# Four quarters of weight preparation and seven weight fetches of the last product group, moved within an order written out by hand

## Chip, core and metric

One core of one Trainium2 chip. The metric is the device time of one execution in microseconds (us).

## The reference

`x` is [16, 512, 512], `router_logits` [16, 512, 8], `expert_weights` [8, 512, 2048], the output [16, 512, 2048], all f32. There are T = 8192 tokens.

```python
probs = softmax(router_logits, axis=-1)
output = zeros((16, 512, 2048))
for e in range(8):
    output += probs[:, :, e:e+1] * np.matmul(x, expert_weights[e])
```

Written as one product, the left matrix is z = (p_e * x) with 8 x 512 = 4096 columns, the right one is the eight weight matrices on top of each other. Both are rounded to f16; sums of products are kept in f32.

## The kernel before

**The products.** The kernel uses Strassen's scheme in Winograd's form, with seven products of half blocks in place of eight. At the top it has 16 pairs q of token blocks (256 rows each, an even and an odd one), two halves of the experts and two halves of the output columns. This gives seven product groups P1 to P7, each a left sum of z blocks times a right sum of weight quadrants. `product(r, q)` (`Product`, `left_of`) is group r for pair q. Each of these is again made of seven inner products in the order `STEPS = (1, 5, 6, 2, 7, 3, 4)` (L353), and an inner product is 8 matmuls of 128x512 f16. The inner operands 1, 2 and 3 of a weight group are raw blocks of it; 5, 7, 6 and 4 are differences of raw blocks. "Thirds" stages (`Thirds` L511, `by_thirds` L781) split the inner products 1 and 5 of two neighbouring pairs a third time; for that `third_sums` (L178) makes four more sums from an operand.

**The stages.** A list of stages sets the order of PE's work. The groups follow one another: P1 and P2 (stages 0 to 14), P5 and P6 (15 to 31), P7 (32 to 39, k7 = 32), P4 (40 to 47, k4 = 40), P3 (48 to 56, k3 = 48). Most stages hold two products and have 14 slots, each one inner product long (the planner counts 1.73 us); stage 48 holds one product and has 7. P4's stages and P3's from 50 on are thirds stages, in which the first four slots run in `by_thirds`. `run(stage)` goes through the slots; `at(stage, slot, make)` hangs a piece of other work in front of a slot.

**What waits for what.** Every engine works in order of its program. DVE's pieces (z operands, weight sums) lie in a queue of `Task`s with a cost in us; `slack` lets as many out after each inner product as the planner's clock for DVE allows, and `need` forces one out when PE's next operand depends on it. ACT copies PSUM results (L595 to L616, L818 to L822) and also issues the fetches of weight operands from DRAM (`fetch_w`, L162 to L164, queue q10 in the profile, 1 MB each). SP issues the loads (`sp`, L117 and L118, q1): blocks of x and p, stored z, and the "base" blocks, earlier results of 256 KB that an adding step (`post_on_base`) adds. GpSimd issues the casting weight loads, stores of weight parts, and the output's stores (`pool`, L120 and L121, q0). All DVE sums go through `tt` (L107), all matmuls through `mm` (L130). Buffers come from `wpool` (15 of 1 MB), `zpool` (8) and `hpool` (12).

**P4's loads.** A product of P4 adds to output rows that P6 and P7 wrote, so `base_at` fetches four base blocks of 256 KB for each; its z of the other expert half is loaded from `z_dram` (`ZBlock`, 1 MB), as is P3's. Loads of a stage are begun two stages ahead (`start_loads`), unless `by_hook` gives them a place.

**P3's weights.** `by_parts` (L1070) makes the seven inner operands of a group in four parts, each a quarter of the rows: `begin` casts four pieces of the raw blocks (`cast_part(22)`, four POOL loads), `go_on` nine slots later stores three of them (`keep_raw`), and `end` sixteen slots after the beginning queues the four sums with their stores (`sums_in_place` L1031). The places are (stage, slot) pairs; `spread(stage, slot, every, n)` counts n places that lie `every` slots apart. `turnover` (L1127) fetches the seven finished operands, in the order of STEPS, at the slots named, counted from the start of a stage. `load_z` (L1151) hangs the z load of a product at a place, and `make_third` (L1158) the third sums of P3's operands 1 and 5. P3's operand fetches are issued by ACT between its copies; its z loads by SP.

Of the kernel before, what the change touches and what calls it, by code (L numbers as in the profile page):

```python
# [31 lines left out]
def kernel(  # L32
# [87 lines left out]
    def pool(o, i, **how):  # L120
        note(nc.gpsimd.dma_start(out=o, in_=i, **how))  # L121
# [12 lines left out]
    def new_w():  # L134
        return wpool.tile([P, K8, NB], f16, name="w", tag="w")
# [26 lines left out]
    def fetch_w(what, kn):  # L162
        t = new_w()
        note(nc.scalar.dma_start(out=t, in_=stored[what, kn]))  # L164
        return t
# [12 lines left out]
    def third_sums(w):  # L178

        t = new_w().rearrange("p (s c) (h n) -> p s c h n", s=2, h=2)  # L180
        t = {5: t[:, 0, :, 0], 6: t[:, 0, :, 1], 7: t[:, 1, :, 0], 4: t[:, 1, :, 1]}
        b = w.rearrange("p (k c) (h n) -> p k c h n", k=2, h=2)
        tt(t[5], b[:, 0, :, 1], b[:, 0, :, 0], SUB)
        tt(t[6], b[:, 1, :, 1], t[5], SUB)
        tt(t[7], b[:, 1, :, 1], b[:, 0, :, 1], SUB)
        tt(t[4], b[:, 1, :, 0], t[6], SUB)
        return {**t, 1: b[:, 0, :, 0], 2: b[:, 1, :, 0], 3: b[:, 1, :, 1]}
# [182 lines left out]
    def flush(task):  # L370
        while task is not None and not task.done:
            queue.popleft().run()
# [6 lines left out]
    def later(cost, make, first=False):  # L379
        t = Task(cost, make)  # L380
        (queue.appendleft if first else queue.append)(t)
        return t
# [286 lines left out]
    def at(stage, slot, make):  # L669
        hooks.setdefault((stage, slot), []).append(make)  # L670

    def add(*products):
        stages.append(products)
        return len(stages) - 1
# [37 lines left out]
    def product(r, q, **how):  # L712
        left, loads = left_of(r, q)
        lefts[r, q] = left
        p = None
        if r == 1:
            def sink(tn, o):
                pool(kept_rows(q)(tn), o)
            p = Product(right[1], left, sink)
        elif r == 2:  # L720
            if q >= QK:
                base = products[1, q].o.__getitem__
            else:
                base = bases[2, q] = Base(kept_rows(q))
            p = Product(right[2], left, to_out(q, 0, 0), base)
        elif r == 5:
            bases[6, q] = m1 = Base(kept_rows(q))
            m1.task = {}

            p = Product(right[5], left, to_out(q, 1, 0))  # L730
        elif r == 6:
            m1 = bases[6, q]

            def base(tn):
                need(m1.task[tn])
                return m1.t[tn]
            p = Product(right[6], left, to_out(q, 0, 1), base)
        elif r == 7:
            base = bases[7, q] = base_of(q) if q < 14 else products[6, q].o.__getitem__
            p = Product(right[7], left, to_out(q, 1, 1), base)  # L740
        elif r == 4:
            base = bases[4, q] = Base(lambda tn: out_rows(q, 1, 1, tn))
            p = Product(right[4], left, to_out(q, 1, 0, accum_op=ADD), base)
        else:
            p = Product(right[3], left, to_out(q, 0, 1, accum_op=ADD), **how)
        p.loads = loads
        products[r, q] = p
        return p
# [150 lines left out]
    k7, k4 = ks[7], ks[4]  # L899
    xs.clear()  # L900
    k3 = add(product(3, 0))
# [129 lines left out]
    def sums_in_place(part, b, r, cost):  # L1031

        def one(p, o, x, y):
            def make():
                tt(o, x, y, SUB)
                part(p, o)
            return later(cost, make)
        one(5, b[0, 0], b[0, 1], b[0, 0])
        one(7, b[0, 1], b[1, 1], b[0, 1])
        one(6, b[1, 1], b[1, 1], b[0, 0])  # L1040
        return one(4, b[1, 0], b[1, 0], b[1, 1])
# [16 lines left out]
    def slots_after(stage, slot, n):  # L1058
        slot += n
        while slot >= 7 * len(stages[stage]):  # L1060
            slot -= 7 * len(stages[stage])
            stage += 1
        return stage, slot

    def part_of(what, kn, chunks):
        return kept_w(what, kn)[:, chunks, :]
# [3 lines left out]
    def by_parts(places, r, load, between, when):  # L1070

        for j, (stage, slot) in enumerate(places):
            b, chunks = {}, ds(2 * j, 2)

            def begin(b=b, j=j, chunks=chunks):
                flush(last_part[0])
                t = new_w()
                for i, kn in enumerate(ORDER):
                    b[kn] = t[:, ds(2 * i, 2), :]
                    load(b[kn], kn, j, chunks)  # L1080

            def go_on(b=b, chunks=chunks):
                for kn in b:
                    if kn != ODD:
                        between(b[kn], kn, chunks)

            def end(b=b, chunks=chunks):
                last_part[0] = sums_in_place(lambda p, o: pool(part_of((r, p), (0, 0), chunks), o), b, r, 0.69)
            at(*slots_after(stage, slot, 0), begin)
            if between is not None:  # L1090
                at(*slots_after(stage, slot, when[0]), go_on)
            at(*slots_after(stage, slot, when[-1]), end)

    def cast_part(q):
        def load(t, kn, j, chunks):
            k, n = kn
            pool(t, expert_weights[(q // 10 - 1) * HE + 2 * k + j // 2, ds(j % 2 * 2 * P, 2 * P),
                                   ds((q % 10 - 1) * NH + n * NB, NB)].rearrange("(c p) n -> p c n", p=P))
        return load
# [18 lines left out]
    def spread(stage, slot, every, n=4):  # L1118
        return [slots_after(stage, slot, j * every) for j in range(n)]
    by_parts(spread(k5 + 2, 4, 13), 7, load_part("t3"), None, (7,))  # L1120
    by_parts(spread(*slots_after(k5 + 2, 4, 56), 28), 4, load_p4, less_t2, (9, 20))
    by_parts([(k4 - 4, 4)] + spread(k4, 4, 26, 3), 3, cast_part(22), keep_raw, (9, 16))


    RAW = {1: (0, 0), 2: (1, 0), 3: (1, 1)}
# [1 line left out]
    def turnover(stage, slots, r, raw):  # L1127

        right[r].w = {}

        def fetch(p):
            if p in RAW:
                right[r].w[p] = fetch_w(raw, RAW[p])
            else:
                right[r].w[p] = fetch_w((r, p), (0, 0))
        for slot, p in zip(slots, STEPS):
            at(*slots_after(stage, slot, 0), lambda p=p: fetch(p))
    turnover(k6 - 1, range(2, 15, 2), 7, "t3")
    turnover(k4 - 1, range(0, 13, 2), 4, "t4")
    turnover(k3 - 1, (1, 2, 5, 6, 7, 8, 11), 3, "b22")  # L1140

    for q in range(16):
        z_dram[q] = dram.tile([P, 2 * K8, HQ], f16, name=f"z_{q}")
# [7 lines left out]
    def load_z(stage, slot, r, q):  # L1151
        load = products[r, q].loads[-1]
        load.by_hook = True
        at(stage, slot, load.begin)
# [3 lines left out]
    def make_third(stage, slot, r, p):  # L1158
        def make():
            third_of[r][p] = third_sums(right[r].w[p])  # L1160
        at(stage, slot, lambda: third_made[r].append(later(2.76, make)))
    at(k6 - 1, 5, lambda: queue_left(lefts[7, 14]))
    make_third(k4 - 1, 7, 4, 1)
    make_third(k4 - 1, 9, 4, 5)
    load_z(k3 - 1, 0, 3, 0)
    load_z(k3 - 1, 12, 3, 1)
    load_z(k3 - 1, 13, 3, 2)
    make_third(k3 - 1, 9, 3, 1)
    make_third(k3 - 1, 10, 3, 5)


    finish = products[3, 15]
# [84 lines left out]
```

## Time and profile before

| | |
|---|---|
| median of 3 runs | 1379.8 us (1379.31 to 1384.13) |
| the profiled execution | 1382.55 us |
| its span | 1380.8 us |
| mean granted clock of TensorE | 0.996 |
| moved by DMA | 388.44 MB, 281 GB/s on the mean |

The span is what the profiler saw from first to last instruction; the execution's own time is longer by what lies around it. PE's stages start in this profile, in us: 44 at 1074.56, 45 at 1100.52, 46 at 1124.02, 47 at 1151.33, 48 at 1174.71, 49 at 1195.64, 50 at 1224.05.

How to read the rows shown below: a row of a timeline has the start, the duration, the engine, the line of the kernel, the operation, output and inputs by the program's names, their shapes, how many instructions were taken together, and in brackets how long the engine stood idle before it and what ended that. A row of the waits has engine, tile and line that waited, what released it, the total, how often, and the longest (in us). A queue's row has packets, MB, and the time of its packets as a share of 16 DMA engines. Rows of DMA issues have count, KB each, and the median us from issue to landing.

### The profile page before, as it was taken

To read this page: it belongs to the slowest core of one execution; us is meant where nothing else is said; L and a number is where in the kernel's file an instruction comes from. 1 tells how busy PE (TensorE), PEld (TensorE's weight loads), DVE (VectorE), ACT (ScalarE), POOL (GpSimd) and SP (SyncE) were. 2 spreads that over 40 slices of the span, in tenths; PEclk is the share of its full clock that TensorE was granted. 3 is DMA by queue.
4 is the path that set the end of the run, shared out by engine and by line. 5 is a ranking of instruction groups with operands and counts; after the bars stand their busy time and mean duration, and the time that the engine had idled before them with its cause. 6 is when DMAs were issued, how large, how long until landed. Compare 5 with 4: busy or idle time off the path is not lost.

```text
span 1380.8 us, 18720 instructions
## 1 busy us (share of the span) xinstructions
PE 1361.1 (99%) x6798; PEld 662.9 (48%) x6798; DVE 1120.3 (81%) x1386; ACT 227.6 (16%) x453; POOL 410.9 (30%) x652
## 2 busy tenths in 40 slices
PE   9999999999999999999999999999999999799998
PEld 4555444444444444444444444444565555256554
DVE  7877767579789887887978888889889888788884
ACT  3232111100011111111111000000121111133331
POOL 3223233331222333323331112221343432123231
PEclk9999999999999999999999999999999999999999
DMA  9999999999899999999998999997999999999976
GB/s 186 231 236 231 211 262 248 260 284 389 251 293 287 331 338 312 310 278 297 333 282 291 404 395 383 279 352 284 307 257 272 266 277 295 326 313 249 217 109 124
DMA packets 199230, 388.44 MB, mean 281 GB/s; under 512 B 53728, under 2 KB 87776, under 8 KB 191584
## 3 DMA queue, kind: packets, MB, share of 16 engines
q0 software_dynamic: 88688, 185.12, 55.7%
q1 hardware_dynamic: 106416, 173.68, 39.2%
q10 hardware_dynamic: 4032, 28.44, 5.2%
q8 instruction: 53, 0.87, 0.2%
q14 instruction: 41, 0.34, 0.1%
HBM read 241.21 MB, written 173.21 MB: 300 GB/s over the span
## 4 chain that ended last, share of the span: by engine, by line
PE 90%; DMA 5%; issue 2%; POOL 1%; DVE 1%; ACT 0%; ACTq 0%; POOLq 0%; DVEq 0%
PE ps L130 67%; PE pt L130 23%; DMA h<-out_dram 2%; DMA wd<-w 1%; POOL out_dram L121 1%; DMA w<-in_expert_weights_dram 1%; DVE z L107 1%; DMA w<-z 1%; DVE w L107 0%; POOL w L121 0%; DVE h L107 0%; DVE ps L107 0%; POOL wd L121 0%; DVE d L107 0%; ACT ps L595 0%
## 5 line engine op out<-in xcount | busy, mean ns | idle before, releaser
L130 PE MATMUL ps<-w,z 128*128 128x512 f16 (+1 forms) x3760 | 824.4, 376 | 11.5 <-DVE z L107 10.0
L130 PEld LDWEIGHTS <-z 128*128 128x128 f16 x5280 | 517.1, 98 | 599.5 <-DVE z L107 12.3
L121 POOL DMA_DIRECT2D out_dram<-h x352 | 231.9, 684 | 681.1 <-ACT h L616 294.9
L130 PE MATMUL pt<-w,z 128*128 128x512 f16 (+1 forms) x1520 | 324.2, 361 | 1.0 <-DVE ps L107 0.6
L107 DVE TENSOR_TENSOR h<-ps,h 128x512 f32<-128x512 f32 x269 | 182.9, 688 | 138.5 <-PE ps L130 112.5
L107 DVE TENSOR_TENSOR z<-xT,pT 128x2048 f16<-128x2048 f16 x220 | 266.5, 1218 | 1.9 <-issue 0.8
L130 PE MATMUL ps<-w,d 128*128 128x512 f16 x880 | 199.3, 379 | 1.2 <-ACT ps L595 1.2
L130 PEld LDWEIGHTS <-d 128*128 128x128 f16 x880 | 86.1, 98 | 101.6 <-issue 1.5
L107 DVE TENSOR_TENSOR z<-z,d 128x2048 f16<-128x2048 f16 x110 | 132.4, 1217 | 0.0
L107 DVE TENSOR_TENSOR w<-w 128x1024 f16<-128x1024 f16 (+2 forms) x116 | 116.4, 1016 | 4.7 <-DMA w<-wd 1.7
L603 ACT COPY h<-ps 128x512 f32<-128x512 f32 x90 | 52.7, 586 | 369.2 <-PE ps L130 358.3
L107 DVE TENSOR_TENSOR h<-pt,h 128x512 f32<-128x512 f32 x111 | 76.2, 688 | 36.4 <-PE pt L130 30.8
L616 ACT COPY h<-ps 128x512 f32<-128x512 f32 x57 | 33.4, 586 | 364.4 <-PE ps L130 348.3
L107 DVE TENSOR_TENSOR z<-z,w 128x2048 f16<-128x2048 f16 x60 | 73.5, 1225 | 8.2 <-DMA w<-z 6.2
L107 DVE TENSOR_TENSOR d<-z 128x1024 f16<-128x1024 f16 x110 | 74.7, 684 | 0.8
L107 DVE TENSOR_TENSOR ps<-ps,h 128x512 f32<-128x512 f32 (+1 forms) x77 | 48.4, 629 | 20.1 <-PE ps L130 15.9
L121 POOL DMA_DIRECT2D wd<-w x86 | 48.7, 578 | 52.3 <-DVE w L107 31.5
L121 POOL DMA_DIRECT2D w<-in_expert_weights_dram x65 | 48.3, 754 | 50.7 <-DMA wd<-w 29.9
L130 PEld LDWEIGHTS <-w 128*128 128x128 f16 x528 | 49.0, 98 | 7.8 <-DMA w<-in_x_dram 1.2
L121 POOL DMA_DIRECT2D kept<-h x56 | 30.8, 551 | 67.5 <-ACT h L603 35.1
L599 ACT COPY h<-ps 128x512 f32<-128x512 f32 x63 | 35.4, 600 | 74.9 <-PE ps L130 73.8
L107 DVE TENSOR_TENSOR h<-h 128x512 f32<-128x512 f32 (+2 forms) x69 | 45.2, 675 | 0.1
(79 smaller groups left out, 430.6 us busy)
## 6 DMA issues: line engine op xcount, KB each, us to landing
out_dram<-h POOLq DMA_DIRECT2D x352, 256.0 KB, 7.8
w<-z SPq DMA_DIRECT2D x30, 1024.0 KB, 12.3
pT<-p_dram SPq DMA_DIRECT2D x108, 256.0 KB, 9.4
w<-wd ACTq DMA_DIRECT2D x27, 1024.0 KB, 10.0
h<-kept SPq DMA_DIRECT2D x100, 256.0 KB, 6.9
h<-out_dram SPq DMA_DIRECT2D x96, 256.0 KB, 12.4
wd<-w POOLq DMA_DIRECT2D x72, 256.0 KB, 8.5
xT<-x SPq DMA_DIRECT2D x71, 256.0 KB, 10.1
```

What stands on the lines that cost most here:

```text
L107: dve(nc.vector.tensor_tensor(out=o, in0=a, in1=b, op=op))
L121: note(nc.gpsimd.dma_start(out=o, in_=i, **how))
L130: note(nc.tensor.matmul(ps, z, w, start=start, stop=stop, skip_group_check=True))
L599: act(nc.scalar.copy(o[tn], q if p == 5 else x))
L603: act(nc.scalar.copy(o[TN[p]], b if p == 2 else x))
L616: act(nc.scalar.copy(o[tn], b))
```

## The change

Nothing is computed differently; four lists of places are changed.

```diff
-    by_parts([(k4 - 4, 4)] + spread(k4, 4, 26, 3), 3, cast_part(22), keep_raw, (9, 16))
+    by_parts(spread(k4 - 7, 4, 42, 2) + spread(k4 + 1, 4, 32, 2), 3, cast_part(22), keep_raw, (9, 16))
...
-    turnover(k3 - 1, (1, 2, 5, 6, 7, 8, 11), 3, "b22")
+    turnover(k3 - 2, (4, 12, 15, 19, 20, 21, 24), 3, "b22")
...
-    load_z(k3 - 1, 0, 3, 0)
-    load_z(k3 - 1, 12, 3, 1)
-    load_z(k3 - 1, 13, 3, 2)
-    make_third(k3 - 1, 9, 3, 1)
-    make_third(k3 - 1, 10, 3, 5)
+    load_z(k3 - 2, 8, 3, 0)
+    load_z(k3 - 1, 11, 3, 1)
+    load_z(k3 - 1, 12, 3, 2)
+    make_third(k3 - 1, 8, 3, 1)
+    make_third(k3 - 1, 9, 3, 5)
```

Worked out as (stage, slot):

| | before | after |
|---|---|---|
| parts 0 to 3 of P3's weights begin | (36,4), (40,4), (42,2), (44,0) | (33,4), (36,4), (41,4), (43,8) |
| fetch of operand 1, operand 5 | (47,1), (47,2) | (46,4), (46,12) |
| fetch of operands 6, 2, 7, 3, 4 | (47,5), (47,6), (47,7), (47,8), (47,11) | (47,1), (47,5), (47,6), (47,7), (47,10) |
| load of z for products (3,0), (3,1), (3,2) | (47,0), (47,12), (47,13) | (46,8), (47,11), (47,12) |
| third sums of operands 1 and 5 | (47,9), (47,10) | (47,8), (47,9) |

## The prediction

> **What bounds the kernel now.** I read the page's part 1, then the waits of PE, the stretches of PE's lost time, the chain of waits, and the DMA queues.
>
> ```profile
> PE 1361.1 (99%) x6798; PEld 662.9 (48%) x6798; DVE 1120.3 (81%) x1386; ACT 227.6 (16%) x453; POOL 410.9 (30%) x652
> PE ps L130 <- DVE z L107: 10.0, 4, 4.4
> ...
> 1065.00:1110.00 45.00, 42.92 (x254) 24.38 (x252) 37.45 (x55) 7.00 (x18) 19.86 (x26) 1.00 1.07 262
> 1110.00:1138.00 28.00, 27.20 (x154) 14.86 (x152) 22.66 (x33) 5.26 (x12) 8.59 (x11) 1.00 1.09 283
> 1138.00:1151.00 13.00, 11.72 (x47) 5.05 (x48) 10.98 (x15) 0.00 (x0) 5.98 (x8) 0.87 1.09 216
> 1151.00:1175.00 24.00, 24.00 (x141) 13.56 (x140) 19.11 (x26) 3.91 (x10) 6.38 (x8) 1.00 1.05 345
> 1175.00:1212.00 37.00, 27.87 (x113) 11.45 (x112) 25.68 (x29) 6.31 (x11) 5.60 (x7) 0.91 1.06 328
> ```
>
> PE is busy in 1361.1 of 1380.8 us, so only the idle 19.7 us and the time at a lower clock are to be had. The stretches (length, then busy time of PE, PEld, DVE, ACT, POOL, then PE's clock, DMA share, GB/s) show where. The second half of P4 (1065 to 1151) idles 2.08 + 0.80 + 1.28 = 4.2 us, and 13 us at a mean clock of 0.87 cost another 1.7: **5.9 us**. The turnover from P4 to P3 (1175 to 1212) idles 9.13 and loses 37 x 0.09 = 3.3 at its clock: **12.4 us**. Everything else the change can only worsen. The DMA engines are full in all five rows.
>
> The turnover's cause is one pair of loads:
>
> ```profile
> 1151.61 26.86 DMA h<-out_dram
> ...
> 1178.59 0.69 DVE L107 TENSOR_TENSOR h<-ps,h 128x512 f32<-128x512 f32 x1 [5.70 <-DMA h<-out_dram]
> ...
> 1178.91 0.57 ACT L595 COPY ps<-ps 128x512 f32<-128x512 f32 x1 [8.22 <-DMA h<-out_dram]
> ...
> 1183.09 0.69 DVE L107 TENSOR_TENSOR h<-ps,h 128x512 f32<-128x512 f32 x1 [1.28 <-DMA h<-out_dram]
> ...
> 1181.26 1.89 PE L130 MATMUL ps<-w,z 128*128 128x512 f16 x8
> ...
> 1187.50 3.49 PE L130 MATMUL ps<-w,z 128*128 128x512 f16 x8 [4.35 <-DVE z L107]
> ...
> 1192.04 1.22 DVE L107 TENSOR_TENSOR z<-z,w 128x2048 f16<-128x2048 f16 x1 [3.46 <-DMA w<-z]
> ...
> 1199.91 2.57 PE L130 MATMUL ps<-w,z 128*128 128x512 f16 x8 [2.38 <-DVE z L107]
> ```
>
> P4's last two base loads (256 KB each, issued by SP at 1151.61 and after) land after 26.9 us and later. DVE, in order, stands still for the first until 1178.59 and for the second until 1183.09; ACT's queue holds a weight fetch that waits for the first, and a ready copy behind it; SP's z load for product (3,1) waits for the second, and lands at 1192. PE's last stall ends at 1199.91, 16.8 us after the second load freed DVE; 3.46 of these are the wait for z, the other 13.3 are DVE at work.
>
> Why two small loads take that long:
>
> ```profile
> q10 hardware_dynamic: 899, 6.59, 48.0%
> q0 software_dynamic: 1022, 1.87, 30.6%
> q1 hardware_dynamic: 1196, 2.95, 26.1%
> ...
> h<-out_dram SPq DMA_DIRECT2D x2, 256.0 KB, 28.6
> ```
>
> In 1151 to 1184 the three queues (packets, MB, share) get through about as many packets each, but ACT's q10 moves 7.3 KB in one and SP's q1 2.5: the seven 1 MB weight fetches take the time, and the z of (3,0), 1 MB, stands ahead of the base loads in q1.
>
> **The change, part by part.** The instruction lists of the two built programs hold equal instructions and equal numbers of them on all engines; PE's order is the same. Everything is a matter of place.
>
> (1) One quarter of P3's weights (part) moves from stage 40 to stage 33. A part is 4 cast loads, 3 raw stores and 4 sums with their stores. In P4 parts 2 and 3 now begin at stages 41 and 43 instead of 40, 42 and 44.
>
> ```profile
> 1076.40 2.86 DVE L107 TENSOR_TENSOR w<-w 128x1024 f16<-128x1024 f16 x4
> ...
> 1135.28 0.68 DVE L107 TENSOR_TENSOR w<-w 128x1024 f16<-128x1024 f16 x1
> 1136.80 0.69 DVE L107 TENSOR_TENSOR h<-ps,h 128x512 f32<-128x512 f32 x1 [0.84 <-DMA wd<-w]
> 1137.40 0.68 DVE L107 TENSOR_TENSOR w<-w 128x1024 f16<-128x1024 f16 x1
> 1138.00 2.36 DVE L107 TENSOR_TENSOR z<-z,d 128x2048 f16<-128x2048 f16 x2
> ...
> 1139.28 7.04 PE L130 MATMUL ps<-w,z 128*128 128x512 f16 x24 [2.07 <-DVE z L107]
> ...
> DVE h L107 <- PE ps L130: 3.3, 8, 0.4
> DVE ps L107 <- PE pt L130: 2.8, 3, 1.6
> ...
> DVE h L107 <- DMA h<-out_dram: 7.7, 7, 1.7
> DVE h L107 <- DMA wd<-w: 3.3, 2, 2.5
> ```
>
> The sums cost DVE 2.86 us a part and stand right ahead of what PE waits for at 1139.28. From 1000 to 1055 DVE's waits (total, times, longest) name PE alone, the first two of these rows; from 1055 to 1140, the last two, they name base loads and stores: the second part uses up the loads' lead, the third finds none. With two parts the stage-44 part is gone; its DVE work at 1135 leaves (1.37 us ahead of a 2.07 us wait), and the last raw stores end about 20 us sooner. Bounds: nothing (the second part still uses up the lead) to all 5.9. I take **4.9**, since the first of the three parts cost PE nothing and the last two will now follow a stretch without one.
>
> (2) In P7 the part adds 2.86 us of DVE, 11 POOL issues, and 4 casts (last row below: 11.3 us to landing). Part 0 of before, three stages later in P7, shows it:
>
> ```profile
> 810.00:835.00 25.00, 25.00 (x118) 11.30 (x116) 21.12 (x25) 1.17 (x2) 4.43 (x9) 1.00 1.03 383
> ...
> 885.00:910.00 25.00, 25.00 (x117) 11.33 (x116) 21.43 (x26) 1.17 (x2) 8.76 (x15) 1.00 1.07 327
> 910.00:935.00 25.00, 25.00 (x117) 11.36 (x116) 23.22 (x29) 1.17 (x2) 6.59 (x13) 1.00 0.97 338
> ...
> w<-in_expert_weights_dram POOLq DMA_DIRECT2D x4, 256.0 KB, 11.3
> ```
>
> There PE lost nothing while POOL cast and DVE summed (23.22 of 25). DVE's 3.9 free us at 810 hide the new part's sums; POOL's queue has 20 free us. The loads of z and base behind it in P7 run a stage or more ahead. Price **0**, at most 2.9 if DVE's slack were gone.
>
> (3) The fetches of P3's operands 1 and 5 (2 MB, ACT's queue) and z of (3,0) (1 MB, SP's queue) move into stage 46.
>
> ```profile
> DMA packets 914, 1.85 MB, mean 185 GB/s; under 512 B 111, under 2 KB 111, under 8 KB 913
> ...
> q0 software_dynamic: 672, 1.41, 95.4%
> q1 hardware_dynamic: 241, 0.43, 14.4%
> ```
>
> From 1140 to 1150 q1 and q10 move almost nothing (185 GB/s in all against 345 later): there is room. 3 MB at 345 GB/s is 8.7 us. In 1151 to 1184 q10 then has five fetches instead of seven and q1 lacks z's packets. At q10's 1 MB in about 4.7 us (6.59 MB in 33 us at 48%, paced by its waits), the two base loads should land 4 to 9 us sooner; none sooner is the lower bound. I take **5.4**: the second at 1177.6. The z of (3,1) then waits for an older load, not for the base load, and the 3.46 us go: **8.9** together, of 12.4. What is late next is the same second base load, about 2.5 us after PE would want its successors, and the rest of DVE's 13.3.
>
> (4) A new wait: the fetch of operand 6 stays in ACT's queue between two copies of P4's last stage, and now waits for a base load that was queued behind z of (3,0).
>
> ```profile
> 1153.28 0.37 ACT L822 COPY keep<-pt 128x256 f32<-128x256 f32 x1
> 1153.54 0.33 ACTq L164 DMA_DIRECT2D w<-wd  x1
> 1153.91 0.37 ACT L822 COPY keep<-pt 128x256 f32<-128x256 f32 x1 [0.26 <-PE pt L130]
> ```
>
> Behind it stands the keep copy of 1153.91, and PE's product (5,7) and DVE's next add wait for that. Before, the fetch went through at once. If PE comes 4.9 us sooner and the load doesn't, ACT is held that long. From 0 to 4.9 for a load as quick as before, with no bound but rival C below; I take **4.5**, near the upper end, because the load now follows 1 MB more.
>
> Moving the third sums and the later z loads by one slot: nothing, they stay behind the same base loads on DVE.
>
> The clock: eight matmuls without a wait take 1.89 us (1181.26), 3.49 after an idle of 4.35 and 2.57 after one of 2.38. I keep the last stall's 1.7 in the rest of the turnover. The Trainium skill (TensorE: Matmul & The Clock Gate, What's actually happening) has the clock halved after at least one idle window of about 3.4 us. The trace does not agree in that: 2.38 us was enough. By the page's rule short stalls would cost no clock and the sum would be 1.7 lower.
>
> **Sum**, against the profiled execution: 1382.55 us, of which 1380.8 are the span. 4.9 + 8.9 - 4.5 - 0 = 9.3 saved: 1373.2. That execution lies 2.75 above the median of the runs, 1379.8; for the median: **1370.5**.
>
> **Rivals.**
>
> ```profile
> h<-out_dram SPq DMA_DIRECT2D x96, 256.0 KB, 12.4
> ```
>
> A, *all stalls go* (0.10): base loads land in the 12.4 us that is their median over the whole span (the page's part 6, above), and nothing holds ACT. 5.9 + 12.4 - 1 = 17.3 saved: 1362.5. For it: the two stretches without a third part lost nothing. Against it: five 1 MB fetches still run beside the base loads.
> B, *the gain is eaten* (0.23): DMA share is 1.05 to 1.09 in P4 and the turnover alike, so what is fetched sooner delays P4's own loads and stores by as much; P4's 5.9 stay, the base loads land as before, and only z's wait of 3.46 goes: 1376.3. The Trainium skill (DMA: Bandwidth & Descriptors, Issuing engines are not separate DMA queues) speaks for this one: all queues run on the same 16 engines and interleave. The shares above agree; the 185 GB/s stretch speaks against the queues being full in each moment.
> C, *ACT is held long* (0.15, the slower side): the base load of (4) starves behind z and the fetches as the pair of before did, 28.6 us. Issued near 1148, it would land near 1177 instead of by 1153.5, and ACT with it: 23 us of PE in stage 47. The turnover's 12.4 would be gone by then and about 2 of P4's: 23 - 14.4 = 8.6 slower, 1388.4. It decides from a landing about 15 us later than before on; slower by over 0.5% from 21 on. Against it: only two fetches are out then, and one of the two is due before it.
> D, *P7 pays* (0.06): DVE's 2.86 and a held buffer show on PE: 9.3 - 2.9 = 6.4 saved, 1373.4.
>
> **How the numbers follow.** Forecast 0.46, A 0.10, B 0.23, C 0.15, D 0.06. About 0.5% (6.9 us) is what a measurement of this kernel tells from no change. The forecast's own range is 1364 to 1376 (the base loads 4 to 9 sooner, ACT held 0 to 4.9, P4's 0 to 5.9). Faster: 0.38 of the forecast's 0.46, A, and 0.03 of D: 0.51. Slower: 0.12 of C, and 0.02 of B for a P4 that gets worse: 0.14. Same: the remaining 0.08, 0.21, 0.03 and 0.03: 0.35. The range for 8 in 10 goes from A to a little beyond B: 1362 to 1381; left out are C's 0.12, B's 0.02 and an A below 1362, 0.05.
>
> **What would show it.** Right: PE without idle time in P7; in P4's stages 44 to 46 no add of DVE waiting for stores of parts; ACT's copy of the last P4 stage waiting a few us for h<-out_dram; the last two base loads landing in 18 to 25 us; no wait of DVE for z of (3,1). Wrong: PE idle time in stages 33 to 36 (D); base loads of 27 us again (B); a gap of PE over 10 us at the copies behind the fetch of operand 6 (C). I would be wrong altogether if P3's later stages, which lost nothing before, stalled for z.

## The result, and the profile after

The changed kernel takes 1377.64 us (median of 20 runs, 1375.92 to 1380.78), the kernel before 1380.87 (20 runs, 1377.75 to 1386.48). The ratio is 0.9973, interval 0.9963 to 0.9984: 3.7 us faster (2.2 to 5.1), where 9.3 had been forecast. The profiled execution took 1376.16 us, 6.4 less than that of before; of these, 1.5 are that it lies below the median of its own runs, and 1.7 that the one of before lies above.

Page part 1 and the waits of PE of the changed kernel:

```profile
PE 1357.2 (99%) x6798; PEld 663.1 (48%) x6798; DVE 1119.8 (81%) x1386; ACT 228.1 (17%) x453; POOL 411.6 (30%) x652
...
PE pt L130 <- ACT keep L822: 8.6, 1, 8.6
PE ps L130 <- DVE z L107: 2.2, 1, 2.2
```

Four waits for DVE's z, 10.0 us in all, have become one of 2.2, and a new one of 8.6 stands in one piece: PE waits for a copy of ACT. The same stretches as in the prediction, and 75 us of P7 (columns as there):

```profile
1065.00:1110.00 45.00, 45.00 (x265) 25.84 (x264) 36.62 (x54) 7.59 (x19) 19.13 (x25) 1.00 1.09 257
1110.00:1138.00 28.00, 25.84 (x148) 14.03 (x146) 23.94 (x33) 4.67 (x11) 8.91 (x11) 1.00 1.07 282
1138.00:1151.00 13.00, 12.40 (x74) 7.05 (x72) 11.89 (x17) 1.46 (x4) 5.53 (x7) 1.00 1.05 288
1151.00:1175.00 24.00, 16.01 (x77) 8.45 (x77) 12.76 (x17) 2.53 (x6) 2.58 (x3) 0.79 1.01 345
1175.00:1212.00 37.00, 36.80 (x171) 16.62 (x170) 33.31 (x40) 7.57 (x13) 10.43 (x13) 1.00 1.07 306
860.00:935.00 75.00, 75.00 (x349) 33.96 (x348) 66.63 (x80) 3.52 (x6) 20.81 (x37) 1.00 1.03 361
```

The turnover (1175 to 1212) is whole, P7 lost nothing, and 1151 to 1175, where nothing was lost before, now idles 8 us and runs at a clock of 0.79. The timeline of ACT and PE there:

```profile
1148.69 0.37 ACT L822 COPY keep<-pt 128x256 f32<-128x256 f32 x1
1158.20 0.33 ACTq L164 DMA_DIRECT2D w<-wd  x1
1158.57 0.37 ACT L822 COPY keep<-pt 128x256 f32<-128x256 f32 x1 [9.50 <-DMA h<-out_dram]
...
1158.99 1.01 PE L130 MATMUL pt<-w 128*128 128x256 f16 x4 [8.59 <-ACT keep L822]
```

The fetch of operand 6 stands between two copies of P4's last stage and waits 9.50 us for a base load; the copy behind it, and PE, wait with it. A weight fetch waits for a base load because of a semaphore, the counter by which a transfer tells that it has landed. The loads of SP and the fetches of ACT share eight of them in turn. In the trace this fetch carries the same one as the base load issued at 1147.69, and ACT's wait for it ends when that load has landed, at 1158.1. In all runs here the fetch goes out only behind the landing of the transfer that had its semaphore before; no run changed the semaphore alone. The chain of waits shows what made the two remaining stalls:

```profile
1089.21 14.09 DMA out_dram<-h
...
1103.35 6.86 DMA h<-out_dram
...
1112.81 10.53 PE ps L130 x48
...
1147.69 10.44 DMA h<-out_dram
```

An output store takes 14.09 us; when it has landed, its buffer is free and SP issues a base load into it (1103.35), and PE resumes after that, at 1112.81, in stage 45. The last part of the weights, begun at (43,8), casts from 1065.4 on and stores until 1119; the last store of the part of (41,4) has just landed at 1065.4, and nothing was lost beside that part. The last row is the load that held ACT. DVE's side of the stall at 1112.81:

```profile
1107.47 0.68 DVE L107 TENSOR_TENSOR w<-w 128x1024 f16<-128x1024 f16 x1
1110.33 0.69 DVE L107 TENSOR_TENSOR h<-ps,h 128x512 f32<-128x512 f32 x1 [2.18 <-DMA h<-out_dram]
1110.94 0.68 DVE L107 TENSOR_TENSOR w<-w 128x1024 f16<-128x1024 f16 x1
1111.54 2.35 DVE L107 TENSOR_TENSOR z<-z,d 128x2048 f16<-128x2048 f16 x2
```

Two sums of the last part (`w<-w`) stand among the adds, as they did before at 1135. The one at 1107.47 ends before the base load lands; the one at 1110.94 stands between the base load and PE's z, so by these rows about 0.6 of the stall is that sum by estimate, and the rest the late load. No run moved the sums apart from the stores.

One more measure is used below. PE's **lost time** is, over all matmuls, the time between two starts beyond the usual 0.216 us (512 columns) or 0.109 (256); it holds idle time and a slow clock. The start of the kernel loses 3.5 to 5.1 in all runs, and is left out. The lost time of a row comes from one profiled execution, which can lie some us off the median of its runs: e3's lies 4.0 below, h3's 2.3 and f1's 2.5 above, and the changed kernel's 1.5 below. The ratio comes from all runs of a kernel, against runs of the kernel before made along with them; the figures in brackets further on are its 95% interval.

(The expectations below, written before the runs, put the stall of 1112.81 in stage 46; it is in stage 45, as above.)

| kernel | P7's end | P4 to stage 46 | held copy, stage 47 | turnover | ratio to before |
|---|---|---|---|---|---|
| before | 0 | 6.6 | 0 | 13.1 | 1 |
| changed | 0 | 2.5 | 10.9 | 0.4 | 0.9973 |
| changed, once more (h3) | 0 | 6.3 | 10.9 | 0.4 | 0.9975 |
| e1 | 0 | 6.0 | 0 | 15.0 | 0.9998 |
| e2 | 0 | 11.2 | 10.2 | 4.0 | 1.0025 |
| e3 | 0 | 3.5 | 0 | 7.1 | 0.9964 |
| e4 | 0 | 5.0 | 0 | 7.6 | 0.9956 |
| f1 | 7.8 | 0 | 1.5 | 8.9 | 0.9980 |
| f2 | 6.2 | 0 | 3.5 | 9.2 | 0.9985 |
| f3 | 4.9 | 0 | 0.5 | 16.1 | 1.0013 |
| f4 | 7.1 | 0 | 0 | 7.7 | 0.9966 |
| g1 | 0 | 5.3 | 0 | 10.6 | 0.9960 |
| g2 | 0 | 0 | 8.8 | 0.5 | 0.9915 |
| g3 | 0 | 0 | 0 | 7.3 | 0.9906 |
| g4 | 0 | 5.5 | 0 | 1.8 | 0.9905 |
| h1 | 0 | 0 | 0.4 | 16.8 | 0.9972 |
| h2 | 0 | 0 | 1.5 | 7.0 | 0.9923 |
| h4 | 0 | 0 | 0 | 9.3 | 0.9918 |

### The profile page after: what moved, and what is told of

The parts are those of the page before. It is cut to its first block, busy times and chain, and to the rows that moved or that the text cites. A ratio compares the mean times of both kernels' runs of the same rounds, so it can differ in the third digit from the quotient of the medians.

```text
span 1374.5 us, 18713 instructions
## 1 busy us (share of the span) xinstructions
PE 1357.2 (99%) x6798; PEld 663.1 (48%) x6798; DVE 1119.8 (81%) x1386; ACT 228.1 (17%) x453; POOL 411.6 (30%) x652
## 4 chain that ended last, share of the span: by engine, by line
PE 92%; DMA 5%; issue 2%; POOL 0%; DVE 0%; ACT 0%; ACTq 0%; POOLq 0%; DVEq 0%; SPq 0%
PE ps L130 69%; PE pt L130 23%; DMA out_dram<-h 3%; DMA h<-out_dram 1%; DMA w<-in_x_dram 0%; POOL out_dram L121 0%; DVE h L107 0%; POOL wd L121 0%; DVE z L107 0%; DVE z L255 0%; DVE w L107 0%; POOL w L121 0%; ACT keep L822 0%; ACT h L1201 0%; ACTq L164 0%
## 5 line engine op out<-in xcount | busy, mean ns | idle before, releaser
L107 DVE TENSOR_TENSOR h<-ps,h 128x512 f32<-128x512 f32 x269 | 182.6, 687 | 124.4 <-PE ps L130 110.7
L107 DVE TENSOR_TENSOR z<-xT,pT 128x2048 f16<-128x2048 f16 x220 | 266.3, 1217 | 4.7 <-issue 3.2
L107 DVE TENSOR_TENSOR z<-z,d 128x2048 f16<-128x2048 f16 x110 | 132.3, 1217 | 0.0
L107 DVE TENSOR_TENSOR w<-w 128x1024 f16<-128x1024 f16 (+2 forms) x116 | 116.4, 1016 | 6.3 <-DMA w<-wd 4.6
L107 DVE TENSOR_TENSOR h<-pt,h 128x512 f32<-128x512 f32 x111 | 76.0, 687 | 33.7 <-PE pt L130 28.6
L107 DVE TENSOR_TENSOR d<-z 128x1024 f16<-128x1024 f16 x110 | 74.5, 684 | 0.8
L107 DVE TENSOR_TENSOR z<-z,w 128x2048 f16<-128x2048 f16 x60 | 73.5, 1225 | 2.0
L107 DVE TENSOR_TENSOR ps<-ps,h 128x512 f32<-128x512 f32 (+1 forms) x77 | 48.4, 629 | 20.2 <-PE ps L130 15.7
L107 DVE TENSOR_TENSOR h<-h 128x512 f32<-128x512 f32 (+2 forms) x69 | 45.2, 675 | 0.1
```

What stands on the lines that cost most here:

```text
L107: dve(nc.vector.tensor_tensor(out=o, in0=a, in1=b, op=op))
```

## The experiments

**e1, the parts alone.**

```diff
-    by_parts([(k4 - 4, 4)] + spread(k4, 4, 26, 3), 3, cast_part(22), keep_raw, (9, 16))
+    by_parts(spread(k4 - 7, 4, 42, 2) + spread(k4 + 1, 4, 32, 2), 3, cast_part(22), keep_raw, (9, 16))
```

> The kernel before with the new places of the four weight parts alone; fetches, z loads and third sums stay where they were. PE's lost time (gaps between matmuls beyond their usual 0.216 or 0.109 us, clock included) was 6.6 us in P4 and 13.1 in the turnover before, 2.5 and 0.4 after, with 10.9 at the held copy. Theory 1 (the parts' gain stands by itself): P4 loses 2.5, the turnover 13, so 4.1 us less than before, ratio 0.997. Theory 2 (the base loads of the turnover land when the queues let them, whatever PE does): P4 loses 2.5 and the turnover about 17, no change, ratio 1.000.

Measured: 0.9998 (0.9982 to 1.0015), no change. The waits of PE:

```profile
PE ps L130 <- DVE z L107: 7.0, 2, 4.1
PE ps L130 <- DVE h L107: 4.3, 1, 4.3
PE ps L130 <- ACT ps L595: 2.5, 1, 2.5
```

Neither theory has the place: P4 itself did not gain. What went before 1100 and in stage 46 came back in stage 45, where a wait for z (4.1) comes behind the last part's stores, as in the changed kernel; stage 47 begins at 1150.9, 0.4 sooner than before. The turnover lost 1.9 more (15.0).

**e2, the fetches, z loads and third sums alone** (the changed kernel with the old `by_parts` line of e1).

> The changed kernel with the parts back at their old places: only fetches, z loads and third sums are moved. Theory 1 (the hold of ACT is the landing of a base load less the time at which ACT comes to the fetch): PE comes to stage 47 as late as before, 4.6 us later than in the changed kernel, so the hold is about 5 us instead of 9.5 and costs 6 with its clock; P4's 6.6 stay, the turnover loses under 1; 6.6 + 6 + 0.5 = 13 of lost time against 20 before, ratio 0.995. Theory 2 (a third of the raw stores and casts ahead of the base load make it as late as PE): hold of 9 us or more, lost time 18 to 20, ratio 0.999 to 1.000.

Measured: 1.0025 (1.0010 to 1.0040), slower.

```profile
PE pt L130 <- ACT keep L822: 7.3, 1, 7.3
PE ps L130 <- DVE z L107: 5.9, 3, 3.5
PE pt L130 <- DVE ps L107: 3.2, 2, 2.9
```

With the old part places the moved fetches and z cost P4 itself 4.6 us more (11.2 instead of 6.6). PE came to stage 47 4.1 us later than before (1155.4) and was still held 7.3. Theory 1 falls: the landing is no fixed time. The base load on the fetch's semaphore was issued only at 1159.1, after ACT had come to the fetch, landed at 1165.5, and the fetch went 0.1 later. The stores of the last part, begun at (44,0), for which the fetch waits too, had landed by 1150.3.

**e3, no copy behind the fetch of operand 6** (the changed kernel and one place).

```diff
-    turnover(k3 - 2, (4, 12, 15, 19, 20, 21, 24), 3, "b22")
+    turnover(k3 - 2, (4, 12, 18, 19, 20, 21, 24), 3, "b22")
```

> The changed kernel with one place changed: the fetch of P3's operand 6 at the end of stage 47's thirds (47,4) instead of between its copies (47,1), so that no copy of these stands behind it. Theory 1 (the hold is a cost of its own): the 10.9 us go and little comes back, 1366 to 1369 us where the changed kernel has 1377.6, ratio to before 0.990. Theory 2 (the hold stands in for the turnover's wait: the last base loads landed at 1166, and PE and DVE would want them from about 1154 on): PE waits at the turnover for 8 to 11 us, within 2 us of the changed kernel, ratio 0.997.

Measured: 0.9964 (0.9948 to 0.9981), not to be told from the changed kernel's 0.9973. The hold of 10.9 is gone, and the turnover loses 7.1 instead of 0.4, in an execution 4.0 below the median of its runs. DMA issues of 1151 to 1184, in the changed kernel and then in e3:

```profile
h<-out_dram SPq DMA_DIRECT2D x2, 256.0 KB, 11.1
```

```profile
h<-out_dram SPq DMA_DIRECT2D x2, 256.0 KB, 18.8
...
1177.69 0.69 DVE L107 TENSOR_TENSOR h<-ps,h 128x512 f32<-128x512 f32 x1 [3.76 <-DMA h<-out_dram]
```

A held ACT issues no fetches. Freed, it sends them beside the last two base loads, which then take 18.8 us instead of 11.1, and DVE waits for these. Theory 2 holds in the main: hold and turnover stand in for each other.

**e4, z of (3,0) back** (the changed kernel).

```diff
-    load_z(k3 - 2, 8, 3, 0)
+    load_z(k3 - 1, 0, 3, 0)
```

> The changed kernel with the load of z of product (3,0) back at (47,0), behind P4's base loads instead of ahead of two pairs of them. Operand 6's fetch then follows operand 5's fetch on its lane (issued at 1144.6) and not a base load. Theory 1 (z ahead makes the hold): base loads take about 5 us again as in the kernel before (5.0 to 5.5 there, 10.4 to 12.0 after), ACT is held until operand 5 lands, 1152 to 1154, so 3 to 5 us instead of 9.5; 4 to 6 us less than the changed kernel if z for (3,0) is not late. Theory 2 (the room is used up by whatever is fetched): hold plus turnover stay at 11 us, within 2 us of the changed kernel.

Measured: 0.9956 (0.9939 to 0.9973), 2 us below the changed kernel, with intervals that overlap. No hold at all, where theory 1 had 3 to 5; 7.6 lost at the turnover, now partly on the operands themselves:

```profile
PE ps L130 <- DVE z L107: 3.1, 1, 3.1
PE ps L130 <- DMA w<-wd: 2.9, 1, 2.9
PE pt L130 <- DMA w<-wd: 2.7, 1, 2.7
```

It doesn't tell the theories apart by time: the fetch of operand 6 shares its semaphore here with another transfer (operand 5's fetch), which the move changed beside z's place.

**f1 to f4, all four parts in P7.** f1 is the changed kernel with this line, f2 adds e4's, f3 is the kernel before with this line alone, f4 is f1 with e3's.

```diff
-    by_parts(spread(k4 - 7, 4, 42, 2) + spread(k4 + 1, 4, 32, 2), 3, cast_part(22), keep_raw, (9, 16))
+    by_parts(spread(k4 - 7, 4, 21, 4), 3, cast_part(22), keep_raw, (9, 16))
```

> The changed kernel with all four weight parts in P7, begun at (33,4), (34,11), (36,4) and (37,11), none in P4; everything else as in the change. Theory 1 (a part in P4 makes the stores of its neighbours slow, 14 us instead of 7.8, these hold the base blocks' buffers, and so the base loads start late): P4 loses under 0.5 us instead of 2.5 to 6.0; the base load that holds ACT lands as long after its issue as with the stores gone, about 7 us instead of 10.4, but PE comes 2.5 sooner, so the hold is 8 to 9; 1373 to 1375, ratio 0.994. Theory 2 (what P4 gives, the turnover takes, since the fetched weights land at about 1186 to 1190 whatever comes first): hold and turnover lose 13 to 14, ratio 0.997 as the changed kernel.

> As the run with all four parts in P7, and the load of z of product (3,0) back at (47,0). Theory 1: P4 loses under 0.5, the turnover 7.6 as with the z back alone (e4), ratio 0.992. Theory 2: the turnover takes what P4 gives, about 12 us in all, ratio 0.9956 as e4.

> The kernel before with all four parts in P7; fetches, z loads and third sums in their old places. Theory 1: P4's 6.6 us go, the turnover keeps its 13, since its fetches are issued by ACT between PE's slots and so come sooner with them: 6 less, ratio 0.9955. Theory 2: turnover 18 to 20, ratio 1.000, as the run with two parts moved (0.9998).

> As the run with all four parts in P7, and the fetch of operand 6 at (47,4) as in e3, so that no copy of the thirds stands behind it. Theory 1: P4 under 0.5, no hold, turnover 7 as in e3: 0.991 to 0.992. Theory 2: turnover of 10 or more, ratio 0.996 to 0.997.

Measured: 0.9980 (0.9965 to 0.9994), 0.9985 (0.9970 to 0.9999), 1.0013 (0.9999 to 1.0028), 0.9966 (0.9948 to 0.9985). In all four P4 loses nothing, as theory 1 said: without a part, no stall in it. But 4.9 to 7.8 us appear in P7's last stages, which neither theory had, and in f1 to f3 hold and turnover together lose 10.4 to 16.6. In f1:

```profile
984.65 2.62 DVE L107 TENSOR_TENSOR w<-w 128x1024 f16<-128x1024 f16 x4 [4.19 <-DMA wd<-w]
...
987.93 1.01 PE L130 MATMUL pt<-w,z 128*128 128x256 f16 x4 [4.99 <-DVE base L107]
...
q0 software_dynamic: 2796, 6.65, 46.4%
q1 hardware_dynamic: 2388, 4.72, 29.3%
q10 hardware_dynamic: 721, 5.25, 29.0%
```

The fourth part, begun at (37,11), meets the turnover from P7 to P4. From 940 to 985 (last rows) q0 moves 6.65 MB beside 5.25 MB of P4's operands. The sums at 984.65 are the third sums of P4's operand 1: they are made in a buffer that was the fourth part's, wait 4.19 until its last store has landed, and the base add behind them on DVE lets PE wait 4.99. It is a stall of the same kind as P4's: a buffer held by a store that takes long (12.9 here).

**g1, fetches behind the base loads** (e3 with four fetches later).

```diff
-    turnover(k3 - 2, (4, 12, 18, 19, 20, 21, 24), 3, "b22")
+    turnover(k3 - 2, (4, 12, 18, 22, 23, 24, 26), 3, "b22")
```

> e3 with the fetches of operands 2, 7, 3 and 4 three to four slots later, (47,8), (47,9), (47,10) and (47,12), so that ACT issues them behind the last base loads. Theory 1 (the fetches crowd the base loads out: these took 17.6 and 20.0 us in e3, 11.7 and 10.4 in the changed kernel, where the held ACT kept the fetches back): the last two base loads land in 10 to 13 us, the turnover loses 3 to 4 instead of 7.1, unless the late operands hold PE; ratio 0.993 to 0.994. Theory 2 (the queues have so much to move by 1187 in any order): the operands land later than they are wanted, PE waits for w<-wd instead, turnover 7 or more, ratio 0.9964 as e3 or worse.

**g4, four fetches left out** (e3; operands 2, 7, 3 and 4 are not fetched, operand 6's data stands in for them).

```diff
+            if r == 3 and p in (2, 7, 3, 4):
+                right[r].w[p] = right[r].w[6]
-            if p in RAW:
+            elif p in RAW:
```

> e3 without the fetches of operands 2, 7, 3 and 4, whose products take operand 6's data in their place (4 MB of 7 left out). Theory 1 (the fetches beside them make the base loads late): the last two base loads land in 8 to 12 us instead of 17.6 and 20.0, the z of (3,1) follows, the turnover loses under 1.5 us instead of 7.1; 1370 to 1372, ratio 0.992. Theory 2 (the base loads are late from their buffers or from the stores): 17 us or more to landing, turnover 6 or more, ratio 0.996.

Measured: g1 0.9960 (0.9944 to 0.9977), as e3; g4 0.9905 (0.9886 to 0.9924). The base loads of 1151 to 1184 in g1, then in g4:

```profile
h<-out_dram SPq DMA_DIRECT2D x3, 256.0 KB, 21.2
```

```profile
h<-out_dram SPq DMA_DIRECT2D x3, 256.0 KB, 12.3
```

g4 shows the cause: without 4 MB of fetches the last two base loads take 12.3 and 12.4 us, where e3 has 17.6 and 20.0, and the turnover loses 1.8. g1 missed: the base loads are issued at 1157.0 and 1158.5 and land at 1178.2 and 1182.6; the fetch of operand 6, issued behind them at 1160.7, overtakes them all the same and lands at 1169.7, and the later operands don't help. The edit moved little: ACT issues the fetch of operand 2 at 1163.3, where e3 has 1161.6.

**g2 and g3, three parts in P7, one in P4's first stage.** g2 is e4 with the line below, g3 is g1 with it.

```diff
+    by_parts(spread(k4 - 7, 4, 21, 3) + [(k4, 4)], 3, cast_part(22), keep_raw, (9, 16))
```

> e4 (z of product (3,0) back at (47,0)) with the weight parts at (33,4), (34,11), (36,4) and (40,4): three in P7, one in P4's first stage, where a part cost PE nothing before. Theory 1 (a part costs where DMA has no lead left: P4's end, or four of them in P7 with the loss at 984 to 994 just when the fourth met the turnover to P4): no loss in P7, none in P4, turnover 7.6 to 9 as in e4 and f2; 3 us less than e4, ratio 0.993. Theory 2 (every part's DMA time comes out somewhere): 4 to 8 us lost at P7's end or in P4's beginning, ratio 0.996 to 0.999.

> Both of the former: parts at (33,4), (34,11), (36,4), (40,4), and the fetch places of g1. Theory 1: no loss in P7 and P4, turnover 3 to 4, ratio 0.990 to 0.991. Theory 2: 0.996 or worse.

Measured: 0.9915 (0.9896 to 0.9935), 1370.4 us, and **0.9906** (0.9889 to 0.9923), 1369.7 us, the fastest whole kernel here. No loss in P7, none in P4: theory 1; the 3 to 4 us that it gave g3's turnover missed. Where the turnover's rest falls differs: g2 is held at the copy (8.8) and loses 0.5 after, g3 is not held and loses 7.3, now to operands that come late. The wait of ACT in g2, then those of PE in g3:

```profile
1154.22 0.37 ACT L822 COPY keep<-pt 128x256 f32<-128x256 f32 x1 [7.54 <-DMA h<-out_dram]
...
PE ps L130 <- DMA w<-wd: 2.8, 1, 2.8
PE pt L130 <- DMA w<-wd: 2.4, 1, 2.4
```

It is e3's exchange once more.

**h1 and h2: the same part places, and nothing else.** h1 is the kernel before, h2 the changed kernel, each with g2's line in place of its own. **h4** is g3 with e4's line; **h3** is the changed kernel itself once more.

> The kernel before with the parts at (33,4), (34,11), (36,4), (40,4) and nothing else. Theory 1 (the parts' places and the fetches have each a worth of their own): P4 loses nothing, the turnover keeps 13 to 16; 3 to 6 us less than before, ratio 0.996 to 0.998. Theory 2 (the parts' places are all there is): 0.991 as g2 and g3. Theory 3 (the turnover takes all that P4 gives, as in the run with two parts moved): turnover 19, ratio 1.000.

> The changed kernel, fetches and all, with only the parts at (33,4), (34,11), (36,4), (40,4). Theory 1: as g2, P4 loses nothing, ACT's copy is held 6 to 9 us, turnover under 2, ratio 0.991 to 0.993. Theory 2 (the z of (3,0) ahead of the base loads is what makes the hold long): the hold is 10 us or more and costs 12, ratio 0.994 to 0.996.

> The changed kernel itself once more. Theory 1 (its stall in stage 46 varies with how the queues fall, and 2.5 us is its low end): 3.5 to 6 us there, hold 8 to 11, profiled execution near 1378; ratio 0.996 to 0.998. Theory 2 (2.5 is this kernel's own figure): 2.3 to 2.7 again, and the profile again 1376.

> g3 with the load of z of product (3,0) back at (47,0). Theory 1 (z out of the way of the base loads helps once nothing holds ACT): turnover 5 to 6 instead of 7.25, ratio 0.989 to 0.990. Theory 2 (the bytes are the same, and z itself is late): turnover 8 to 10, ratio 0.992 or worse.

Measured: h1 0.9972 (0.9958 to 0.9986), h2 0.9923 (0.9907 to 0.9939), h3 0.9975 (0.9962 to 0.9988), h4 0.9918 (0.9898 to 0.9937), theory 2 there in lost time (9.3). In h4 the z load, ahead of the last two base loads again, makes them land in 21.2 us on the median, where g3 has 12.7: z's place, too, is a part of why they are late. h1 came out as its theory 1, with 16.8 at the turnover. h2 has the ratio of its theory 1 and not the places, a hold of 1.5 and a turnover of 7.0. The DMA issues of 1080 to 1112 in the changed kernel, then in h2:

```profile
q0 software_dynamic: 2198, 4.46, 67.0%
...
out_dram<-h POOLq DMA_DIRECT2D x9, 256.0 KB, 14.1
wd<-w POOLq DMA_DIRECT2D x7, 256.0 KB, 12.7
```

```profile
q0 software_dynamic: 1436, 2.61, 54.5%
...
out_dram<-h POOLq DMA_DIRECT2D x10, 256.0 KB, 6.6
```

Without a part there the output stores land in 6.6 us instead of 14.1, and stage 45 has no stall. At the fetch of operand 6, in h2:

```profile
1142.69 6.06 DMA h<-out_dram
...
1149.14 0.37 ACT L822 COPY keep<-pt 128x256 f32<-128x256 f32 x1 [2.21 <-DMA h<-out_dram]
...
PE ps L130 <- DVE h L107: 4.7, 1, 4.7
PE pt L130 <- ACT keep L822: 1.3, 1, 1.3
```

The base load that ACT waits for lands in 6.06 us instead of 10.44, and PE is held 1.3 us instead of 8.6, though z of (3,0) still goes ahead. So in the kernel as changed most of the hold went with the parts in P4's end. A part of that is by chance: in h2 the fetch has the semaphore of the first load of a pair, in the changed kernel that of the second. The second one of h2 landed at 1150.8, 2.0 after the first, so with it the hold would have been about 4.2 on ACT by estimate, not 2.21. And parts in P4's end are not needed for a long hold: g2 has none, z back behind the pair, and the second load of the pair, 9.56 us to landing, held ACT 7.54. In h1, which keeps the old fetches, the chain has

```profile
1145.38 31.59 DMA h<-out_dram
...
PE ps L130 <- DVE h L107: 10.4, 1, 10.4
```

and of the 6.6 us that P4 gave, the turnover took 3.7 (13.1 to 16.8). The fetches are worth 8.7 us of lost time from h1 to h2 (17.2 to 8.5), and 0.49% by the ratios, about 6.8 us.

h3 shows where two executions of the changed kernel differ. Its waits of PE:

```profile
PE pt L130 <- ACT keep L822: 8.7, 1, 8.7
PE ps L130 <- DVE z L107: 4.5, 1, 4.5
```

The same kernel, the same hold, but 4.5 us in stage 45 where the first profile had 2.2: 6.3 lost in P4 against 2.5, and 1379.80 us against 1376.16. In e1, e4, g1 and g4, with the same part places, P4 lost 5.0 to 6.0, in e3 3.5. The first profile has the least of the seven. Neither is the median execution (1377.6), and why the stall varies is not shown.

## Why the prediction was right or wrong

- **(1) P4's parts, 4.9 forecast: wrong, and the step that failed.** It reasoned that "the first of the three parts cost PE nothing and the last two will now follow a stretch without one". e1, the parts alone, measured 0.3 us (2.1 slower to 2.5 faster), and h3's P4 lost 6.3 of the old 6.6; the first profile, with 2.5, comes nearest to the forecast. By these runs the cause is another than the lead of the loads: beside the last part, begun at (43,8), the only one under way then, output stores take 14.1 us instead of 6.6, these hold the base blocks' buffers, and base loads of stage 45 are issued late (h2 against the changed kernel). Why the part of (41,4) cost nothing was not tried by itself. The lower bound, nothing, was right in size, if not for its reason, "the second part still uses up the lead"; the nearest row, three parts of which the first was free, showed a part at P4's beginning, not one at its end. A row was misread as well, "DVE h L107 <- DMA wd<-w: 3.3, 2, 2.5": both adds began 0.1 us behind the landing of a base load (1087.7 and 1136.7), no store of a part landed in the 20 us before either, and what DVE waited for were base loads.
- **(2) P7, price 0: right** for a second part there (75.00 of 75.00 us busy). Three, with the third at (36,4), cost nothing either; a fourth at (37,11) cost 4.9 to 7.8.
- **(3) The turnover, 8.9 saved of 12.4: the mechanism right, the size by luck.** With no part in P4's end it was 8.7 together with its hold (h1 to h2); in the kernel as changed 13.1 became 0.4, but only because PE had stood 10.9 elsewhere, and 7.1 without that (e3). The last two base loads took 11.7 and 10.4 us there, not the 18 to 25 named as a sign, since the held ACT kept the fetches back. The wait for z of (3,1), 3.46, did go. g4 shows that the reason given, fetches beside the base loads, was a reason, and h4 against g3 the other one given, z ahead of them. (The 4.7 us per fetch are 33 / 7; by the 6.59 MB named beside it they would be 5.0.)
- **(4) The hold of ACT, 4.5: place right, the way it was priced wrong.** It is 9.50 on ACT, 8.59 on PE, 10.9 with the clock. Priced was PE's lead, "if PE comes 4.9 us sooner and the load doesn't, ACT is held that long". In the first profile PE came 4.6 us sooner (stage 47 at 1146.8 instead of 1151.3), and the load besides about 4.6 later, at 1158.1 (1147.69 + 10.44) instead of by 1153.5. But in h3 PE came only 0.9 sooner (1150.4) and ACT was held 9.64, and in e2 4.1 later and ACT was held 8.3: the load is issued only when an output store of P4 has landed and freed its buffer, at 1147.6, 1152.8 and 1159.1 in the three, and this moves, too. "There is room" was read from 185 GB/s, though the row of the same stretch has a DMA share of 1.09: in 1130 to 1148 base loads took 12.7 us on the median in the changed kernel, and 6.6 in e1 with the same part places and the old fetches. The hold's price by itself was smaller than its length: with it gone (e3) the time stayed the same within the intervals.
- **The sum.** Lost time before less h3's: P4 0.3, turnover 12.7, hold -10.9, start 0.6, together 2.7, and 1382.55 less 1379.80 is 2.75. Forecast were 4.9, 8.9 and -4.5. Turnover and hold stand in for each other and came to 1.8 where 4.4 were forecast; the larger miss is P4's. With no part in P4's end the fetches gave more than those 4.4 (6.8, h1 to h2), and the whole change 0.9923, about 10.6 us. The low ends that its range names, nothing for P4, 7.5 for the turnover and a hold of 4.9, add up to 2.6 saved, 1377.2, close to the 1377.6 measured; the range of 1364 to 1376 leaves out that they come together.
- **The rivals.** B came nearest, 1376.3 to 1377.6 measured, but mostly by luck. P4's loss did stay, though not for B's reason, the fetches: in e1, which moves none, it stayed too. The moved fetches did delay P4's own loads, as B says, and that cost at the hold; base loads of 27 us as before did not happen. C's mechanism happened at less than half its length: the base load took 10.44 us, not 28.6. A and D did not happen in this kernel; A's end, all but the start's loss gone, no run reached (the least lost here was 7.3, in g3 and g4).
- **The clock.** The prediction took 2.38 us of idle time as enough to slow the matmuls, and before, 24 matmuls after an idle of 2.07 took 7.04 us. After, 48 took 10.53 after an idle of 2.16 (47 x 0.216 + 0.38 = 10.53): no loss at all. After 8.59, four of 256 columns took 1.01, where 0.60 is usual. The Trainium skill (TensorE: Matmul & The Clock Gate, What's actually happening) names an idle window of about 3.4 us; by it the 2.16 would cost nothing, with which this trace agrees, and the 2.07 neither, with which that of before does not.

## What to carry to other kernels

Background transfers have a price that depends on which lead they use up: before a piece of weight preparation is moved, look how long the stores and loads of its new neighbours take to land, since a store that holds a buffer delays the next load into it, and a load delays an engine in order. Two halves of a change are to be measured apart and together; here one gave nothing, the other cost 3.5 us, and both gave 3.7, because the late parts hid what the fetches were worth. Where a profile shows less loss in one stall and a new one elsewhere, take the profile again and take the new stall away: it may only hold the place of the old one.

## What the runs showed of the hardware

The time of one 256 KB transfer follows its neighbours: base loads of the same size took 6.06 us (h2), 10.44 (changed) and 31.59 (h1, beside the 1 MB fetches), and output stores 6.6 us on the median without a weight part in the same queue (h2) and 14.1 with one (changed). How long an idle time of PE must be before its clock falls isn't told by its length alone: 2.07 us slowed it in one profile and 2.16 did not in another.
